# Assembling the attention output of a two-layer hybrid diffusion trunk: two ScalarE copies and one GpSimd add for each half-copied, half-added pair on ScalarE and VectorE

## The chip, the cores and the metric

The kernel runs on one core of one Trainium2 chip. The metric is the device time of one execution in microseconds (us); lower is better. The kernel before takes 2939.41 us, the median of three runs (2939.0 to 2944.37).

## The reference

The reference is a trunk of two layers over 1024 latent tokens and 256 context tokens, 1024 features wide, batch 1, in float32. Layer 0 mixes tokens with a convolution module, layer 1 with grouped-query attention (16 query heads, 4 key/value heads, 64 features each). After each of the two stands a SwiGLU feed-forward network (FFN) with 2816 hidden features. What the change touches is the attention of layer 1, for the latent tokens:

```python
qg = q.reshape(B, Q, N_KV_HEADS, KV_GROUP, Dh)
s = jnp.einsum("bqkgd,bskd->bkgqs", qg, k).astype(jnp.float32) * (Dh ** -0.5)
p = jax.nn.softmax(s, axis=-1).astype(v.dtype)
o = jnp.einsum("bkgqs,bskd->bqkgd", p, v)
...
yx = ob.transpose(1, 0, 2, 3).reshape(B, S, N_HEADS * HEAD_DIM) @ wo
```

The 1024 queries read all 1280 keys (latent and context).

## The kernel before

**Number format.** Large products are made from pairs. A float32 number is split into a high part (rounded to the matmul's faster format) and a low part (the remainder), and a product is the sum of high x high, high x low and low x high. ScalarE makes the high part by a copy, VectorE the low part by a subtraction. TensorE (PE in the profile) does all products and the transposes; its results lie in the eight banks of PSUM, which GpSimd does not read anywhere in this kernel.

**Attention, one unit at a time.** The work of attention is cut into 32 units. A unit is one key/value head with its four query heads, for 128 queries. The scores of a unit (`scores`, line 1105) take 24 matmuls (L1116: four heads, 1280 keys in pieces of 512 and 256, high and low part of the keys). For each head VectorE scales the 1280 scores of a query, takes their minimum and writes them to SBUF (L1122), and ScalarE takes the exponential with the sum beside it (L1124).

The values of a unit (`values`, line 1128) go through the 1280 keys in ten tiles of 128. For each tile PE transposes the four heads' probabilities into one bank (L1134, four instructions), ScalarE copies the high part out of it (L1137), VectorE subtracts to get the low part (L1138), and PE multiplies both by the values (L1140 with the high part, L1141 with the low part) and sums all ten tiles up in one bank, number 7, called `av`. Two banks take the transposes in turn while attention runs alone, one while it shares the core; four slots hold the high and low parts, so at most four tiles can be ahead of the multiplications.

**Putting the output together.** The values' weights hold the high parts of the 64 value features in 64 columns and their low parts in the other 64, so `av` holds in its lower 64 partitions the part of the output that comes from the high parts, and in its upper 64 the part from the low parts, for four heads of 128 queries. The output of a unit is the sum of the two, laid out as 128 partitions (two heads x 64 features) by two by 128 queries, and then divided by the softmax's sums. For each half of the partitions, ScalarE copies one part from `av` to the scratch tile `tmp`, moving it across partitions (L1151, 64 x 256 numbers), and VectorE adds the other part, read from `av`, to it and writes the output tile `dst` (L1152). The reciprocal of the sums is taken by VectorE (L1145), spread out by GpSimd (L1147), transposed by PE into bank 7 (L1155, two instructions, called the two small transposes below), and VectorE multiplies the output by it (L1156). GpSimd then issues the DMA that writes the unit's output to memory (L1450). The last unit of each half of the queries writes to a tile of its own, `olast`, with no DMA. Bank 7 has to be read out by all of this before the next unit's first L1140 may write to it.

**What sets the order.** The Python code is a set of generators that a tile framework's scheduler then lists engine by engine, by its own cost model and by priorities; `later(40)` gives the L1140 and L1141 a lower priority. Each engine executes its list strictly in order and waits at an instruction until the instructions that it depends on are done. So a change of one instruction can change the whole list. GpSimd's list also holds the DMA issues: a unit's queries (L1102), keys (L1095), outputs (L1450), and the loads for the output projection (L1485, L1500).

**Stages of the second layer.** From about 1565 us the first 16 units (queries 0 to 511) start beside the last query/key projections (`qkv`); from about 1640 to 1862 us they run alone. Then the output projection of the first half (`out_proj`, from line 1481) starts on these units' output, and the other 16 units (queries 512 to 1023) run beside it and, from about 1965 us, beside the FFN of the first half, until 2393 us. The rest is the second half's output projection and FFN.

Of the kernel before, what the change touches and what calls it, by code (L numbers as in the profile page):

```python
# [12 lines left out]
ALU = mybir.AluOpType  # L13
# [42 lines left out]
class Kern:  # L56
# [1071 lines left out]
    def values(self, t, Ps, sums, dst, done):  # L1128
        nc, c = self.nc, self.c
        av = self.bank("av")  # L1130
        for j in range(NJ):
            tp = self.bank("pt")
            for h in range(4):
                nc.tensor.transpose(tp[:, h * P:(h + 1) * P], Ps[h][:, j * P:(j + 1) * P], c["ident"])  # L1134
            ph, pl = self.ptring[self.ptslot % len(self.ptring)]
            self.ptslot += 1
            nc.scalar.copy(ph, tp)  # L1137
            nc.vector.tensor_tensor(pl, tp, ph.bitcast(F32), op=ALU.subtract)  # L1138
            with self.later(self.lav):
                nc.tensor.matmul(av, lhsT=self.value(t, j), rhs=ph, start=j == 0, stop=False)  # L1140
                nc.tensor.matmul(av, lhsT=self.value(t, j), rhs=pl, start=False, stop=j == NJ - 1)  # L1141
            yield 0.87

        r = sums[:, 1, :]
        nc.vector.reciprocal(r, sums[:, 0, :])  # L1145
        rx = self.sb(256)
        nc.gpsimd.tensor_copy(rx.rearrange("p (h d) -> p h d", d=HD), r.unsqueeze(2).to_broadcast([P, 4, HD]))  # L1147
        tmp = self.sb(256).rearrange("p (a q) -> p a q", q=P)
        v = av.rearrange("p (a b q) -> p a b q", b=2, q=P)
        for b, r, o in ((0, slice(0, 64), slice(64, 128)), (1, slice(64, 128), slice(0, 64))):  # L1150
            nc.scalar.copy(tmp[r], v[o, :, b, :])  # L1151
            nc.vector.tensor_tensor(dst[r], v[r, :, b, :], tmp[r], op=ALU.add)  # L1152
        rb = self.bank("av")
        for a in range(2):
            nc.tensor.transpose(rb[:, a * P:(a + 1) * P], rx[:, a * P:(a + 1) * P], c["ident"])  # L1155
        nc.vector.tensor_tensor(dst, dst, rb[:, 0:256].rearrange("p (a q) -> p a q", q=P), op=ALU.mult)  # L1156
        done()
        yield 0.1
# [565 lines left out]
```

## Time and profile before

| what | value |
|---|---|
| time, median of 3 runs | 2939.41 us |
| time of the profiled execution | 2938.98 us |
| its span, first to last instruction | 2937.2 us |
| mean granted PE clock in it | 0.987 |
| busy: PE, VectorE (DVE), ScalarE (ACT), GpSimd (POOL) | 97%, 74%, 45%, 8% |
| L1151, ScalarE's copies | 64, 23.5 us in all |
| L1152, VectorE's adds | 64 (60 to scratch tiles, 4 to `olast`) |
| L1147, GpSimd's spreading copies | 32, 13.8 us in all |

All times inside the kernel are counted from the start of the span. In rows that group instructions, the columns are: line, engine, operation, output<-input by the program's names with their shapes, count, then busy time in us and mean duration of one in ns, then idle time of the engine just before them in us and what ended most of it. In rows of a timeline, the columns are: start in us, duration in us, engine, line, operation, output<-input, count, and in brackets the idle time of the engine just before it and what ended it. PE is the stream of matmuls, PEld that of the weight loads ahead of them. Matmuls overlap in the pipeline, so the distance between the starts of two neighbours says what one costs, and not its duration.

### The profile page before, as it was taken

The page shows a single profiled execution, that of the slowest core. Times are in us where ns is not written, and L with a number is a line of the kernel's source. Part 1 is how long each engine was busy: PE and PEld are TensorE (multiplying, and loading weights), DVE is VectorE, ACT ScalarE, POOL GpSimd, SP SyncE. Part 2 cuts the span into 40 slices and gives each one's busy share as a digit, 9 for nine tenths or more (in the row PEclk, how much of TensorE's full clock was granted, in tenths as well). Part 3 has the DMA queues.
Part 4 walks back from the last instruction along what each step waited for, and adds up shares of the span by engine and source line. Part 5 has one row for each costly group of instructions (what it writes and reads, how often), then busy time and mean ns, then how long its engine had stood idle before and what let it go on. Part 6 is the DMA issues. An engine that isn't in the chain of part 4 may idle for free.

```text
span 2937.2 us, 42731 instructions
## 1 busy us (share of the span) xinstructions
PE 2847.7 (97%) x16462; PEld 2446.1 (83%) x16462; DVE 2160.7 (74%) x3746; ACT 1335.5 (45%) x2229; POOL 222.6 (8%) x377
## 2 busy tenths in 40 slices
PE   7999989999999999999999999989999999999998
PEld 6888877888888889989888787767777778889997
DVE  6887788847556378877786899786666666786777
ACT  5222255532222245544445688645555543444444
POOL 0000001011022001000011111110000000010000
PEclk9999999999999999999999999999999999999999
DMA  6443444334356224333345211322222143353332
GB/s 249 140 120 98 116 131 145 135 116 143 115 175 198 65 74 165 114 104 112 109 156 170 88 46 46 97 87 81 66 73 83 60 149 99 110 170 104 102 98 75
DMA packets 131755, 336.58 MB, mean 115 GB/s; under 512 B 31328, under 2 KB 52864, under 8 KB 130656
## 3 DMA queue, kind: packets, MB, share of 16 engines
q1 hardware_dynamic: 78016, 222.33, 24.1%
q0 software_dynamic: 29344, 103.83, 10.7%
q10 hardware_dynamic: 24192, 7.70, 1.1%
q8 instruction: 129, 2.11, 0.3%
q14 instruction: 74, 0.61, 0.1%
HBM read 289.50 MB, written 38.93 MB: 112 GB/s over the span
## 4 chain that ended last, share of the span: by engine, by line
PE 86%; DVE 7%; ACT 2%; issue 2%; DMA 2%; ACTq 0%; POOL 0%; SPq 0%; DVEq 0%; POOLq 0%
PE ps L172 15%; PE ps L173 15%; PE ps L174 15%; PE ps L875 4%; PE ps L877 4%; PE ps L876 4%; PE ps L1116 4%; PE ps L1134 4%; PE ps L1140 2%; PE ps L454 2%; PE ps L455 2%; PE ps L456 2%; PE ps L1141 2%; PE ps L185 1%; PE ps L183 1%
## 5 line engine op out<-in xcount | busy, mean ns | idle before, releaser
L172 PE MATMUL ps<-T,wh 128*128 128x512 f32 (+1 forms) x1360 | 502.5, 370 | 1.4 <-ACT T L161 0.8
L174 PE MATMUL ps<-T,wl 128*128 128x512 f32 (+1 forms) x1360 | 500.4, 368 | 2.0 <-DVE wl L148 2.0
L173 PE MATMUL ps<-T,wh 128*128 128x512 f32 (+1 forms) x1312 | 481.4, 367 | 0.2 <-DVE T L164 0.2
L144 ACT CAST wh<-wr 128x1024 fp32r<-128x1024 f32 (+1 forms) x217 | 225.0, 1037 | 419.9 <-PE ps L173 307.2
L148 DVE TENSOR_TENSOR wl<-wr,wh 128x1024 fp32r<-128x1024 f32 (+1 forms) x217 | 261.9, 1207 | 168.5 <-ACT wh L144 167.1
L875 PE MATMUL ps<-T,wh 128*128 128x256 f32 x1092 | 310.7, 285 | 5.0 <-ACT wh L161 4.5
L876 PE MATMUL ps<-T,wh 128*128 128x256 f32 x1092 | 306.5, 281 | 0.0
L877 PE MATMUL ps<-T,wl 128*128 128x256 f32 x1092 | 305.4, 281 | 0.2 <-DVE wl L164 0.2
L1138 DVE TENSOR_TENSOR T<-ps,T 128x512 fp32r<-128x512 f32 x320 | 216.8, 687 | 107.6 <-ACT T L1137 106.8
L172 PEld LDWEIGHTS ps<-T,wh 128*128 128x128 f32 x1360 | 257.8, 190 | 43.7 <-ACT T L1506 1.7
L174 PEld LDWEIGHTS ps<-T,wl 128*128 128x128 f32 x1360 | 257.7, 190 | 42.4 <-DVE wl L148 2.2
L173 PEld LDWEIGHTS ps<-T,wh 128*128 128x128 f32 x1312 | 248.5, 189 | 38.2 <-DVE T L164 1.3
L1137 ACT CAST T<-ps 128x512 fp32r<-128x512 f32 x320 | 186.0, 586 | 191.1 <-PE ps L1134 177.6
L173 PE MATMUL ps<-HS,wh 128*128 128x512 f32 x656 | 257.9, 393 | 0.0
L172 PE MATMUL ps<-HS,wh 128*128 128x512 f32 x608 | 238.4, 392 | 0.9 <-ACT wh L144 0.9
L174 PE MATMUL ps<-HS,wl 128*128 128x512 f32 x608 | 237.5, 391 | 0.0
L875 PEld LDWEIGHTS ps<-T,wh 128*128 128x128 f32 x1092 | 206.1, 189 | 11.2 <-ACT wh L161 6.7
L876 PEld LDWEIGHTS ps<-T,wh 128*128 128x128 f32 x1092 | 206.6, 189 | 0.5
L877 PEld LDWEIGHTS ps<-T,wl 128*128 128x128 f32 x1092 | 206.2, 189 | 0.6 <-DVE wl L164 0.4
L1134 PE MATMUL ps<-cst,T 128*128 128x128 f32 x1100 | 189.6, 275 | 3.2 <-DVE T L1138 3.1
L1122 DVE TENSOR_SCALAR_CACHE_REDUCE T<-ps,rq 128x1280 f32<-128x1280 f32 x110 | 170.0, 1546 | 27.9 <-PE ps L1116 22.1
L1134 PEld LDWEIGHTS ps<-cst,T 128*128 128x128 f32 x1100 | 132.6, 141 | 49.5 <-DVE T L1138 30.8
(377 smaller groups left out, 6195.9 us busy)
## 6 DMA issues: line engine op xcount, KB each, us to landing
wr<-in_w SPq DMA_DIRECT2D x170, 512.0 KB, 3.6
wr<-in_pw SPq DMA_DIRECT2D x35, 512.0 KB, 3.5
HV<-in_wmodT POOLq DMA_DIRECT2D x56, 256.0 KB, 4.1
q<-in_wmodT POOLq DMA_DIRECT2D x56, 256.0 KB, 3.9
KB<-in_w SPq DMA_DIRECT2D x24, 512.0 KB, 3.6
HR<-in_w SPq DMA_DIRECT2D x23, 512.0 KB, 3.7
q<-in_w SPq DMA_DIRECT2D x23, 512.0 KB, 4.2
q<-qsd POOLq DMA_DIRECT2D x32, 256.0 KB, 3.3
```

The costliest lines, as they stand in the source:

```text
L144: nc.scalar.copy(hi, raw)
L148: nc.vector.tensor_tensor(lo, raw, hi.bitcast(F32), op=ALU.subtract)
L172: nc.tensor.matmul(out[:, :n], lhsT=wh, rhs=xh, start=k == 0, stop=False)
L173: nc.tensor.matmul(out[:, :n], lhsT=wh, rhs=xl, start=False, stop=False)
L174: nc.tensor.matmul(out[:, :n], lhsT=wl, rhs=xh, start=False, stop=k == nk - 1)
L875: nc.tensor.matmul(out, lhsT=wh, rhs=bh, start=first and k == 0, stop=False, **skip)
L876: nc.tensor.matmul(out, lhsT=wh, rhs=bl, start=False, stop=False, **skip)
L877: nc.tensor.matmul(out, lhsT=wl, rhs=bh, start=False, stop=k == 3, **skip)
L1122: nc.vector.tensor_scalar(out=pt, in0=sc, scalar1=rq[:, h:h + 1], scalar2=None, op0=ALU.mult, op1=ALU.min, accum_out=mn)
L1134: nc.tensor.transpose(tp[:, h * P:(h + 1) * P], Ps[h][:, j * P:(j + 1) * P], c["ident"])
L1137: nc.scalar.copy(ph, tp)
L1138: nc.vector.tensor_tensor(pl, tp, ph.bitcast(F32), op=ALU.subtract)
```

## The change

In `values`, the first of the two parts is still copied by ScalarE into `tmp`. The second is no longer added by VectorE on its way out of the bank: ScalarE copies it to `dst` as well, for both halves of the partitions, and then one GpSimd instruction over all 128 partitions adds `tmp` to `dst`, both in SBUF. For a unit, that is four copies on ScalarE and one add of 128 x 256 on GpSimd where there were two copies on ScalarE and two adds of 64 x 256 on VectorE.

```diff
         for b, r, o in ((0, slice(0, 64), slice(64, 128)), (1, slice(64, 128), slice(0, 64))):
             nc.scalar.copy(tmp[r], v[o, :, b, :])
-            nc.vector.tensor_tensor(dst[r], v[r, :, b, :], tmp[r], op=ALU.add)
+            nc.scalar.copy(dst[r], v[r, :, b, :])
+        nc.gpsimd.tensor_tensor(dst, dst, tmp, op=ALU.add)
         rb = self.bank("av")
```

Lines below it move down by one: in the changed kernel L1152 is the second copy, L1153 the add, L1156 the small transposes (L1155 before), L1157 the multiplication (L1156 before), and L1451 the output's DMA (L1450 before).

The scheduler lists the engines anew. Three places show it, all without the number of the row.

**VectorE, at the end of a unit while attention runs alone.** Names: `T_13571` holds the slots of high and low parts, `HS`, `T_13569` and `T_14068` (`T_14069` after) the probabilities, `sb` the scratch and output tiles. Before:

```order
L1122 TENSOR_SCALAR T_13569,mn<-ps,rq_10629 128x1280
L1138 TENSOR_TENSOR T_13571<-ps,T_13571 128x512
L1152 TENSOR_TENSOR sb<-ps,sb 64x256
L1138 TENSOR_TENSOR T_13571<-ps,T_13571 128x512
L1122 TENSOR_SCALAR HS,mn<-ps,rq_10629 128x1280
L1152 TENSOR_TENSOR sb<-ps,sb 64x256
L1138 TENSOR_TENSOR T_13571<-ps,T_13571 128x512
L1156 TENSOR_TENSOR sb<-sb,ps 128x256
L1122 TENSOR_SCALAR T_13569,mn<-ps,rq_10629 128x1280
```

The same unit's end after:

```order
L1138 TENSOR_TENSOR T_13571<-ps,T_13571 128x512 x2
L1122 TENSOR_SCALAR HS,mn<-ps,rq_10629 128x1280
L1138 TENSOR_TENSOR T_13571<-ps,T_13571 128x512 x2
L1145 RECIPROCAL sums<-sums 128x4
L1157 TENSOR_TENSOR sb<-sb,ps 128x256
L1122 TENSOR_SCALAR T_13569,mn<-ps,rq_10629 128x1280
```

The two adds are gone, and the multiplication stands nearer to the unit's last subtraction: one pass over the scores lies between where there were two.

**PE, at the same unit's end.** `HR` and `HV` are the values, `KB` the keys, `cst` the identity of the transposes; the first row's L1141 is the unit's last multiplication, and the next unit's first one is an L1140. Before:

```order
L1141 MATMUL ps<-T_13571,HR 128x512
L1116 MATMUL ps<-KB,q 128x512 x4
L1116 MATMUL ps<-KB,q 128x256 x2
L1116 MATMUL ps<-KB,q 128x512 x2
L1134 MATMUL ps<-cst,T_13569 128x128
L1134 MATMUL ps<-cst,T_14068 128x128 x3
L1116 MATMUL ps<-KB,q 128x512 x2
L1134 MATMUL ps<-cst,T_13569 128x128
L1134 MATMUL ps<-cst,T_14068 128x128 x3
L1116 MATMUL ps<-KB,q 128x256 x2
L1116 MATMUL ps<-KB,q 128x512
L1155 MATMUL ps<-cst,sb 128x128 x2
```

After (the next unit's L1140 is the last row; before, it stands behind two more score matmuls and three more transposes):

```order
L1141 MATMUL ps<-T_13571,HR 128x512
L1116 MATMUL ps<-KB,q 128x512
L1116 MATMUL ps<-KB,q 128x256 x2
L1116 MATMUL ps<-KB,q 128x512 x2
L1134 MATMUL ps<-cst,T_13569 128x128
L1134 MATMUL ps<-cst,T_14069 128x128 x3
L1156 MATMUL ps<-cst,sb 128x128 x2
L1116 MATMUL ps<-KB,q 128x512
L1134 MATMUL ps<-cst,T_13569 128x128
L1134 MATMUL ps<-cst,T_14069 128x128 x3
L1140 MATMUL ps<-T_13571,HV 128x512
```

The small transposes stand after five score matmuls and four transposes where 13 and eight preceded them, and the next unit's first multiplication after six and eight where 15 and 11 preceded it.

**GpSimd, at the end of the first unit.** Before:

```order
L1102 DMA q<-qsd 128x4x128
L1450 DMA od<-sb 128x2x128
L1102 DMA q<-qsd 128x4x128
L1147 COPY sb<-sums 128x256 x2
L1450 DMA od<-sb 128x2x128
```

After:

```order
L1102 DMA q<-qsd 128x4x128
L1153 ISA
L1153 TENSOR_TENSOR sb<-sb 128x256
L1147 COPY sb<-sums 128x256
L1451 DMA od<-sb 128x2x128
L1102 DMA q<-qsd 128x4x128
L1147 COPY sb<-sums 128x256
L1153 TENSOR_TENSOR sb<-sb 128x256
L1451 DMA od<-sb 128x2x128
```

An add stands ahead of each output DMA, and ahead of the first add one more instruction, `ISA`, which tells GpSimd to load the library of code that the add is in; it stands there once.

## The prediction

> **What bounds the kernel now.** The page first, for the share of each engine:
>
> ```profile
> PE 2847.7 (97%) x16462; PEld 2446.1 (83%) x16462; DVE 2160.7 (74%) x3746; ACT 1335.5 (45%) x2229; POOL 222.6 (8%) x377
> ```
>
> PE is busy nearly throughout, so VectorE's 74% says little: what an add less on VectorE is worth depends on whether PE waits there. The adds lie in the second layer's attention, so I cut that into stages with the windows view (columns: stretch, its length, busy us and count of PE, PEld, DVE, ACT, POOL, then granted clock, DMA share, GB/s):
>
> ```profile
> 1640.00:1865.00 225.00, 215.06 (x1281) 174.13 (x1280) 202.94 (x335) 180.24 (x304) 33.93 (x55) 1.00 0.19 53
> 1965.00:2385.00 420.00, 419.31 (x2155) 329.73 (x2154) 278.47 (x407) 229.06 (x357) 29.76 (x47) 1.00 0.26 77
> ```
>
> These are two different kernels. In the first stretch attention runs alone: VectorE is busy 90% of it, ScalarE 80%, and PE has gaps. In the second PE has FFN matmuls to fill every gap and waits 0.7 us in 420; VectorE has a third of its time free. A gain can come from the first stretch only. Its groups over eight units, with shapes kept apart, show who is close to the limit:
>
> ```profile
> L1138 DVE TENSOR_TENSOR T<-ps,T 128x512 fp32r<-128x512 f32 x82 | 54.6, 685 | 8.3 <-ACT T L1137 8.1
> L1137 ACT CAST T<-ps 128x512 fp32r<-128x512 f32 x80 | 46.1, 587 | 19.8 <-PE ps L1134 12.3 <-PE ps L1140 4.9
> ...
> L1152 DVE TENSOR_TENSOR sb<-ps,sb 64x256 f32<-64x256 f32 x16 | 6.7, 416 | 0.2
> ...
> L1151 ACT COPY sb<-ps 64x256 f32<-64x256 f32 x16 | 5.9, 368 | 0.4
> ...
> L1156 DVE TENSOR_TENSOR sb<-sb,ps 128x256 f32<-128x256 f32 x8 | 3.3, 410 | 0.0
> L1147 POOL COPY sb<-sums 128x256 f32<-128x256 f32 x8 | 3.2, 399 | 8.9 <-DMA od<-sb 4.4 <-issue 3.7 <-POOL sb L1147 0.6
> ```
>
> VectorE's idle time in front of its main step (8.3 us in eight units) is spent waiting for ScalarE's high parts, and ScalarE's (19.8 us) waiting for PE: a ring of three engines with short queues, none of them at its limit. The chain of waits gives the pace, by two score passes at the same place of the pattern eight units apart:
>
> ```profile
> 1702.22 1.16 PE ps L1116 x6
> ...
> 1819.87 1.17 PE ps L1116 x6
> ```
>
> That is 117.65 / 8 = 14.71 us a unit. What PE alone would need comes from the spacing of neighbours in the timeline:
>
> ```profile
> 1731.47 1.32 PE L1116 MATMUL ps<-KB,q 128*128 128x512 f32 x6
> ...
> 1732.63 1.03 PE L1134 MATMUL ps<-cst,T 128*128 128x128 f32 x8
> ...
> 1733.42 0.48 PE L1141 MATMUL ps<-T,HR 128*128 128x512 f32 x1
> ...
> 1739.85 0.40 PE L1141 MATMUL ps<-T,HV 128*128 128x512 f32 x1
> ...
> 1740.09 0.39 PE L1140 MATMUL ps<-T,HR 128*128 128x512 f32 x1
> ```
>
> Six score matmuls take 1.16 us, eight transposes 0.79, one multiplication 0.24. A unit has four times the first (4.64), five times the second (3.95), 20 of the third (4.8) and two small transposes of 0.1: 13.6 us. So PE loses 1.1 us a unit here, and no change on another engine can win more than that.
>
> **What goes, what comes, and what is moved.** The stretch holds the ends of units 0 to 14, so 14 distances of a unit. The end of a unit, between its last multiplication and the next unit's first, reads now:
>
> ```profile
> 1734.36 0.37 ACT L1151 COPY sb<-ps 64x256 f32<-64x256 f32 x1
> 1734.63 1.36 ACT L1124 ACTIVATE T<-T,mn 128x1280 f32<-128x1280 f32 x1
> 1734.91 0.40 DVE L1152 TENSOR_TENSOR sb<-ps,sb 64x256 f32<-64x256 f32 x1
> ...
> 1735.84 1.53 DVE L1122 TENSOR_SCALAR_CACHE_REDUCE HS<-ps,rq 128x1280 f32<-128x1280 f32 x1
> ...
> 1736.11 0.36 ACT L1151 COPY sb<-ps 64x256 f32<-64x256 f32 x1
> ...
> 1737.41 0.43 DVE L1152 TENSOR_TENSOR sb<-ps,sb 64x256 f32<-64x256 f32 x1
> ...
> 1738.01 0.39 PE L1155 MATMUL ps<-cst,sb 128*128 128x128 f32 x2
> ...
> 1738.47 0.41 DVE L1156 TENSOR_TENSOR sb<-sb,ps 128x256 f32<-128x256 f32 x1
> ...
> 1738.80 1.54 DVE L1122 TENSOR_SCALAR_CACHE_REDUCE T<-ps,rq 128x1280 f32<-128x1280 f32 x1
> ...
> 1738.94 0.50 PE L1140 MATMUL ps<-T,HV 128*128 128x512 f32 x1
> ```
>
> The two copies and two adds take turns, and an exponential and a pass over the scores slip in between, so bank 7 is held from 1733.42 to 1738.94, 5.5 us.
>
> *Gone:* two adds of 0.416 a unit, 0.83 us of VectorE's busy time. Neighbours overlap by 0.08 (0.41 from 1738.47 on, the next at 1738.80), so I count, with one overlap left out, 0.75 us of VectorE's time a unit.
>
> *Added on ScalarE:* two copies of 0.368. The one above lets its neighbour start 0.27 after it, so four in a row take 3 x 0.27 + 0.37 = 1.18 us, 0.54 more than two. ScalarE is idle 19.8 / 8 = 2.5 us a unit in front of L1137 alone; that covers it. If that cover fails, an exponential comes up to 0.54 later.
>
> *Added on GpSimd:* one add of 128 x 256. The trace has no GpSimd add. The nearest row from below is L1147, a copy of the same shape, one input: 0.40. Two inputs read in turn would be 0.80. I take 0.65, nearer to the upper end, since there are two inputs. [...]
>
> *The chain at a unit's end after.* From the start of the last multiplication to the first copy:
>
> ```profile
> 1863.83 0.40 PE L1141 MATMUL ps<-T,HR 128*128 128x512 f32 x1
> ...
> 1864.26 0.37 ACT L1151 COPY sb<-ps 64x256 f32<-64x256 f32 x1 [0.38 <-PE ps L1141]
> ```
>
> 0.43, then four copies 1.18, then about 0.05 for each hand-over: the small transposes can start at 1.66, the add at 1.66 as well, the multiplication at 1.66 + 0.65 + 0.05 = 2.36, the next unit's first L1140 at 2.36 + 0.41 + 0.05 = 2.8. PE has, by the order shown, six score matmuls (four wide, two narrow: 1.18), eight transposes (0.8) and the two small ones (0.2) in between, 2.2 us behind the 0.24 of the last multiplication. So PE waits 2.8 - 2.4 = 0.4 us there. The order runs in a cycle of three units; at the other two ends, by the same count, there are 3.3 and 3.65 us of matmuls, and PE doesn't wait. That is 0.12 us a unit.
>
> VectorE waits too, since L1157 stands in its queue in front of the next scores and subtractions, and it is reached early: at the end shown one pass of 1.54, two subtractions of 0.685, each less the overlap of 0.08, and a reciprocal (0.1) lie between the unit's last subtraction and it, 2.8 us. The last multiplication starts 0.7 after that subtraction (one tile's transposes, 0.4, and an L1140 go ahead of it), so the multiplication could start 0.7 + 2.36 = 3.1 after it: a wait of 0.3. ScalarE, however, has two L1137 in front of the four copies, which can push them back by up to 0.9. I take the long end, 1.2, because both L1137 wait for an exponential that ends just before: 0.4 us a unit over the cycle of three. At the other two ends two passes over the scores lie between, and the product is ready in time.
>
> Gain a unit: 0.75 - 0.4 - 0.12 = 0.23, say 0.2; over 14 units **-2.8 us**. Bounds: the whole 0.75, so -10.5, if neither wait occurs; +1, if the small waits come at each end.
>
> *At the end of the stretch.* The output of unit 14 goes to memory and comes back for the output projection, and ScalarE and PE wait for it:
>
> ```profile
> 1860.72 0.83 ACT L161 CAST T<-HS 128x768 fp32r<-128x768 f32 x1 [2.05 <-DMA HS<-od]
> ...
> 1862.09 0.50 PE L1140 MATMUL ps<-T,HR 128*128 128x512 f32 x1 [1.18 <-ACT T L1137]
> ```
>
> Unit 14's multiplication now stands ahead of two subtractions that preceded it, so its DMA leaves earlier; of PE's 1.18 I count half: **-0.5** (between 0 and -1.2).
>
> *Once: the library.* GpSimd is free before the first add:
>
> ```profile
> 1637.80 0.77 POOL L1102 DMA_DIRECT2D q<-qsd  x1 [0.61 <-PE ps L1134]
> 1648.04 0.71 POOL L1450 DMA_DIRECT2D od<-sb  x1 [9.47 <-DVE sb L1156]
> ```
>
> ```profile
> 1642.64 0.37 ACT L1151 COPY sb<-ps 64x256 f32<-64x256 f32 x1
> ```
>
> From 1638.57 on it may load, and the first add is due when four copies from 1642.64 on are done, at 1643.8: 5.2 us. No row shows such a load. The nearest are ScalarE's table load and, as the long end, the median landing of a 512 KB DMA:
>
> ```profile
> L1124 ACT ACT_TABLE_LOAD x1 | 1.3, 1283 | 0.0
> ```
>
> ```profile
> q<-in_w SPq DMA_DIRECT2D x23, 512.0 KB, 4.2
> ```
>
> With 1.3 to 4.2 us it is hidden: **0**. If it took longer, each us more would hold the first output, its multiplication in VectorE's queue, and so PE. [...]
>
> *Beside the FFN.* PE is full, so VectorE's relief brings nothing in these 14 unit ends. What can cost is that the small transposes now stand closer behind the last multiplication, in most units after some 1.4 us of matmuls. They need the four copies: 1.66 against 0.24 + 1.4 = 1.64. The row for them before shows that they wait a little already, beside other matmuls:
>
> ```profile
> L1155 PEld LDWEIGHTS ps<-cst,sb 128*128 128x128 f32 x28 | 2.9, 141 | 3.2 <-issue 2.7 <-POOL sb L1147 0.3
> ```
>
> I take 0.05 us an end, **+0.7**; bounds 0, and 0.3 an end (+4.2), if ScalarE is in the middle of an exponential of 1.37 at one end in five. GpSimd's queue holds the adds behind query loads (L1102), which wait for the scores two units back; those stand ahead of the small transposes on PE, so no add waits for one. L1450 and the loads behind it come as late as the add makes them, and nobody waits for an output DMA but the last of each half.
>
> Sum: -2.8 - 0.5 + 0 + 0.7 = -2.6 us. Against the profiled execution, 2938.98 us with a span of 2937.2, this is 2936.4; that execution is 0.43 below the median of the three runs, so I forecast **2936.8 us** for the median.
>
> **The rivals.** About 0.2%, 5.9 us, is what a measurement of this kernel tells from no change.
>
> *VectorE's relief is kept whole.* If VectorE is what paces the ring, the unit shrinks by all of 0.75, which PE's 1.1 of slack allows: -10.5 - 0.5, or 2928.4 us. For it speaks VectorE's 90% and that the exchange over bank 7 falls from 5.5 to some 3 us; against it, that VectorE's idle time is spent waiting for ScalarE, which gets more work. Chance 0.20, counting from 2933.5 down.
>
> *GpSimd's add becomes the wait (the other side).* The chain copies, add, multiplication, next L1140 has no slack at one end in three and 0.9 to 1.2 us at the others. If the add takes 1.4 us instead of 0.65 and hand-overs to and from GpSimd 0.2 each, the chain is 3.9 us and PE loses 1.5, 0.4 and 0 at the three ends, 0.63 a unit, while VectorE waits some 1.0 a unit: a unit is 0.9 longer, over 14 units +12, so 2951 us. It decides from an add of about 1.0 us on, where VectorE's waits eat the 0.75. Against it stands L1147 with 0.40. Chance 0.09.
>
> *ScalarE's copies hold up PE beside the FFN.* If the four copies come behind an exponential of 1.37 at most of the 14 ends, PE waits 0.7 at each, +10, and with -3.3 from the other stage the time is 2946 us. ScalarE is busy 229 of 420 us there, which makes it possible, but the order places them where ScalarE is expected free. Chance 0.05, the long library load included.
>
> That the change does not do what it says is ruled out by the order: 128 copies and 32 adds stand in it.
>
> **How the numbers follow.** The forecast, a time within 5.9 us of 2939.4, has 0.66; of its range, the gain of 10.5 is cut in half and the loss of 4.2 taken beside no gain, so 2933.5 to 2943.5. To hold 8 in 10, the range goes down into the first rival, to 2930; 2943.5 leaves out the two slower ones. Faster by over 0.2%: 0.20. Within 0.2%: 0.66. Slower: 0.09 + 0.05 = 0.14.
>
> **What would show it.** Right: 14.4 to 14.6 us a unit between 1700 and 1820; the add at 0.5 to 0.8 us; VectorE idle for L1157 at one unit end in three, for GpSimd; PE's busy time beside the FFN still within 1% of the stretch; a gap on GpSimd before its first add, over before 1643.8. Wrong: a unit under 14.0 (VectorE did pace the ring), a unit over 14.7 or VectorE waiting for the add at every end (GpSimd is the new wait), or PE waiting for the small transposes by more than 0.3 us each beside the FFN.

## The result and the profile after

The changed kernel takes **2949.41 us**, the median of 11 runs (2945.95 to 2953.03); the kernel before, run beside it, 2940.61 us (2938.53 to 2944.37). The ratio is 1.003 (95% interval 1.0022 to 1.0038): slower by 8.8 us, where I had forecast 2936.8 us, a gain of 2.6. The profiled execution after took 2946.87 us, with a span of 2945.1 us, 7.9 us longer than that of before (2937.2).

The two stages first, by the windows view (columns as in the prediction: stretch, its length, busy us of PE, PEld, DVE, ACT, POOL, granted clock, DMA share, GB/s):

```profile
1640.00:1865.00 225.00, 213.36 (x1268) 173.18 (x1268) 189.20 (x299) 187.84 (x331) 46.31 (x72) 1.00 0.20 55
1965.00:2385.00 420.00, 414.87 (x2128) 326.02 (x2127) 266.38 (x377) 237.13 (x382) 39.05 (x60) 1.00 0.26 76
```

VectorE is relieved in both (202.94 to 189.20, and 278.47 to 266.38). But PE, which was busy 419.31 of 420 us beside the FFN, is now busy 414.87: the stage in which PE had no gap has gaps of 5 us. The waits view names them; first alone (1640 to 1865), then beside the FFN (1990 to 2390). Columns: waiting engine and line, releaser, us in all, times, longest.

```profile
PE ps L1156 <- ACT sb L1152: 6.7, 14, 0.8
...
PE ps L1140 <- DVE sb L1157: 0.7, 4, 0.2
```

```profile
PE ps L1156 <- ACT sb L1152: 4.0, 12, 0.4
```

The second is the only PE wait that the view lists in those 400 us; before, it lists none. L1156 are the small transposes: PE reaches them while ScalarE is still copying `av` out of bank 7, which they write. The timeline shows one such end beside the FFN:

```profile
2071.18 0.48 PE L1141 MATMUL ps<-T,HR 128*128 128x512 f32 x1
...
2071.74 0.37 ACT L1151 COPY sb<-ps 64x256 f32<-64x256 f32 x1 [0.70 <-issue]
...
2072.13 0.37 ACT L1152 COPY sb<-ps 64x256 f32<-64x256 f32 x1
...
2072.88 0.37 ACT L1152 COPY sb<-ps 64x256 f32<-64x256 f32 x1
2073.28 1.37 ACT L1124 ACTIVATE T<-T,mn 128x1280 f32<-128x1280 f32 x1
2073.39 0.41 PE L1156 MATMUL ps<-cst,sb 128*128 128x128 f32 x2 [0.35 <-ACT sb L1152]
...
2074.16 0.42 DVE L1157 TENSOR_TENSOR sb<-sb,ps 128x256 f32<-128x256 f32 x1 [1.47 <-POOL sb L1153]
```

The first copy starts 0.56 us behind the last multiplication, the copies start 0.38 apart and don't overlap (the last L1152 is the fourth copy: 1.51 us for all four), and the small transposes come 2.2 us behind the last multiplication, 0.35 of which PE stands still. The exponential (L1124), whose input VectorE finished at 2072.7, waits behind the copies until 2073.28. VectorE waits 1.47 us for the add, but nothing of PE's stands behind that here.

At the same place the kernel before has the two copies apart, with an exponential between them; ScalarE waits 0.18 us ahead of the first copy and 0.65 behind it, so that one lies in a gap:

```profile
2066.97 0.37 ACT L1151 COPY sb<-ps 64x256 f32<-64x256 f32 x1 [0.18 <-PE ps L1141]
2067.99 1.37 ACT L1124 ACTIVATE T<-T,mn 128x1280 f32<-128x1280 f32 x1 [0.65 <-DVE T L1122]
...
2069.47 0.36 ACT L1151 COPY sb<-ps 64x256 f32<-64x256 f32 x1
```

Where the 7.9 us of the two spans came from is read by the same instruction in both kernels at five places: the first unit's multiplication, the output projection's first square (L390), the FFN's first product (L839), a group of eight tiny matmuls (L746, each one column wide) in the second norm (its first group, HS, is for the clock, below), and the end. The first three rows are of the timeline, the other two of the view by line (duration in ns: least, median, most; then first and last start). Before:

```profile
1647.34 0.41 DVE L1156 TENSOR_TENSOR sb<-sb,ps 128x256 f32<-128x256 f32 x1
...
1883.70 0.64 ACT L390 ACTIVATE sb<-T 128x512 f32<-128x512 f32 x1
...
1966.66 0.68 DVE L839 SCALAR_TENSOR_TENSOR sm<-sm,ps 128x512 f32<-128x512 f32 x1
```

```profile
L746 PE MATMUL ps<-cst,HS x8: 250/250/250, 1933.2 to 1934.0; 128*128 128x1 f32 x8
...
L746 PE MATMUL ps<-cst,HV x8: 250/250/250, 2480.9 to 2481.7; 128*128 128x1 f32 x8
```

After:

```profile
1644.92 0.41 DVE L1157 TENSOR_TENSOR sb<-sb,ps 128x256 f32<-128x256 f32 x1
...
1883.92 0.64 ACT L390 ACTIVATE sb<-T 128x512 f32<-128x512 f32 x1
...
1969.43 0.68 DVE L839 SCALAR_TENSOR_TENSOR sm<-sm,ps 128x512 f32<-128x512 f32 x1
```

```profile
L746 PE MATMUL ps<-cst,HS x8: 352/352/352, 1935.1 to 1936.6; 128*128 128x1 f32 x8
...
L746 PE MATMUL ps<-cst,HV x8: 250/250/250, 2488.0 to 2488.8; 128*128 128x1 f32 x8
```

| stretch | difference at its end | lost in it |
|---|---|---|
| up to the first unit's multiplication | -2.4 | -2.4 |
| alone, with the stage's last unit end, to the first L390 | +0.2 | +2.6 |
| output projection and norm, to the first L839 | +2.8 | +2.6 |
| beside the FFN, to the second L746 | +7.1 | +4.3 |
| the rest | +7.9 | +0.8 |

The first row is not the change's. PE's matmuls stand in the same order in both kernels up to the last multiplication of the first unit, and ahead of it one and the same L1140, first before and then after, comes 2.4 us earlier:

```profile
1633.39 0.51 PE L1140 MATMUL ps<-T,HR 128*128 128x512 f32 x1 [0.45 <-ACT T L1137]
```

```profile
1631.01 0.50 PE L1140 MATMUL ps<-T,HR 128*128 128x512 f32 x1 [0.45 <-ACT T L1137]
```

The lead is 2.4 us at 1548 us already, before the first unit begins, so this execution was ahead by that much for reasons that the change doesn't touch. At the first unit's last multiplication on PE (L1141) it is 3.4 (1641.75 before, 1638.34 after); counted from there the second row is 3.6, not 2.6. From the L1140 on, this pair of profiles differs by 10.3 us, where the medians differ by 8.8.

PE's clock has a part in the rows. In the norm the eight HS matmuls last 352 ns instead of 250. The windows view has the granted clock; before, over three stretches of some 10 us:

```profile
1632.00:1642.00 10.00, 8.11 (x30) 6.21 (x31) 8.01 (x21) 5.13 (x7) 2.22 (x3) 0.66 0.35 131
...
1930.00:1941.00 11.00, 9.94 (x58) 8.00 (x57) 8.91 (x29) 4.16 (x8) 0.00 (x0) 0.84 0.17 55
...
2486.00:2496.00 10.00, 10.00 (x48) 8.14 (x47) 9.72 (x27) 4.58 (x7) 1.68 (x3) 1.00 0.38 131
```

After:

```profile
1632.00:1642.00 10.00, 8.13 (x37) 5.84 (x37) 7.47 (x18) 6.86 (x12) 3.29 (x5) 0.83 0.36 131
...
1930.00:1941.00 11.00, 10.10 (x48) 8.34 (x47) 8.31 (x22) 4.42 (x8) 0.00 (x0) 0.69 0.24 79
...
2486.00:2496.00 10.00, 10.00 (x52) 8.53 (x52) 5.54 (x26) 1.63 (x2) 0.00 (x0) 0.83 0.18 55
```

The two traces hold no other clock than 1 and one half, so this is 6.8, 3.5 and 0 us at half clock before, and 3.4, 6.8 and 3.4 after. At half clock PE's matmuls of 128x512 start 0.43 us apart (2490.27 to 2492.83 after), at the full clock 0.23 (2484.91 to 2486.04), so PE loses at most half of each, and the clock can have given 1.7 us in the first place (the lead grew by 1.0 there) and taken 1.7 in each of the other two. But all stretches at half clock of the two spans add up to 78 us before and 76 after, so the 7.9 as a whole can't be put down to the clock. The largest piece of the loss lies beside the FFN, where the granted clock is 1.00 throughout.

### The profile page after: what moved, and what is told of

Its sections match the earlier page's. It is cut to its first block, busy times and chain, and to the rows that moved or that the text cites. A ratio compares the mean times of both kernels' runs of the same rounds, so it can differ in the third digit from the quotient of the medians.

```text
span 2945.1 us, 42741 instructions
## 1 busy us (share of the span) xinstructions
PE 2849.6 (97%) x16462; PEld 2447.8 (83%) x16462; DVE 2137.4 (73%) x3682; ACT 1357.2 (46%) x2293; POOL 245.8 (8%) x409
## 5 line engine op out<-in xcount | busy, mean ns | idle before, releaser
L1138 DVE TENSOR_TENSOR T<-ps,T 128x512 fp32r<-128x512 f32 x320 | 215.6, 688 | 125.5 <-ACT T L1137 125.3
L1134 PE MATMUL ps<-cst,T 128*128 128x128 f32 x1100 | 189.5, 275 | 3.1 <-DVE T L1138 3.1
L1122 DVE TENSOR_SCALAR_CACHE_REDUCE T<-ps,rq 128x1280 f32<-128x1280 f32 x110 | 170.2, 1548 | 30.6 <-PE ps L1116 24.6
L1134 PEld LDWEIGHTS ps<-cst,T 128*128 128x128 f32 x1100 | 132.7, 141 | 47.5 <-DVE T L1138 28.3
```

The lines of the kernel that those rows point to most:

```text
L1122: nc.vector.tensor_scalar(out=pt, in0=sc, scalar1=rq[:, h:h + 1], scalar2=None, op0=ALU.mult, op1=ALU.min, accum_out=mn)
```

## The experiments

Theory A, from the profile above: the loss comes from four ScalarE copies between a unit's last multiplication and the small transposes, which PE reaches too early. Theory B, the rival: the GpSimd add makes VectorE wait (8.1 us alone, 13.2 beside the FFN), and PE behind it. "Alone" and "beside" in the code are told by the ring of score regions, `sring`.

**One stage at a time.**

```diff
+            if self.sring != [TOK]:
                 nc.scalar.copy(dst[r], v[r, :, b, :])
+            else:
+                nc.vector.tensor_tensor(dst[r], v[r, :, b, :], tmp[r], op=ALU.add)
...
+        if self.sring != [TOK]:
+            nc.gpsimd.tensor_tensor(dst, dst, tmp, op=ALU.add)
```

> The new form only for units that end while two score regions are in use (from some 1640 us to the FFN), the old form for the rest. Theory A (the loss lies beside the FFN, where PE reaches the small transposes 1.4 us behind the last multiplication and waits for four ScalarE copies; the stage alone nets nothing): 2938 to 2942 us, and no PE wait at the small transposes between 1990 and 2390 us. Theory B (the GpSimd add makes VectorE, and PE behind it, wait at each unit's end, mostly alone): 2946 to 2950 us.

Measured: 2954.34 us, ratio 1.0049 (1.0036 to 1.0061). Beside the FFN, as theory A says, nothing is lost:

```profile
1990.00:2390.00 400.00, 399.96 (x2057) 315.06 (x2057) 264.61 (x389) 218.67 (x341) 28.33 (x45) 1.00 0.26 77
```

But alone it loses far more than the changed kernel did, 15.6 us a unit (see the table below), though the instructions at each end are the same on the same engines. What differs is the list: the scheduler, which lists the two stages together, now repeats the shortest of the three unit ends of the changed kernel at every unit, with 2.2 us of matmuls between a unit's last multiplication and the next one's first. PE waits for the small transposes (7.8 us), VectorE for GpSimd (15.1 us at 11 ends):

```profile
PE ps L1160 <- ACT sb L1153: 7.8, 14, 0.6
```

```profile
DVE sb L1161 <- POOL sb L1157: 15.1, 11, 1.4
```

So theory B is not empty: alone, with this list, VectorE waits for the add at 11 ends and a unit is 0.9 us longer than before. The time agrees with neither number. The reverse has `==` for `!=`:

> The reverse: the new form only for the units that end beside the FFN, the old form alone; beside the FFN the list of PE has the same distances as after the change. Theory A: most of the loss is here, 2945 to 2949 us, with PE waiting at the small transposes for ScalarE about 0.35 us at each of 12 ends or more between 1990 and 2390 us, and PE's busy time there 4 us lower than before. Theory B: 2940 to 2942 us, since VectorE has a third of its time free there.

Measured: 2945.94 us, ratio 1.0018 (1.0009 to 1.0027), as theory A says: the form beside the FFN takes most of the loss by itself. Beside the FFN PE stands at the small transposes (L1160 here) for the same 4.0 us at 12 ends:

```profile
PE ps L1160 <- ACT sb L1153: 4.0, 12, 0.4
```

**The add on VectorE, or the copy on VectorE.** These take apart the two things that the change adds.

```diff
-        nc.gpsimd.tensor_tensor(dst, dst, tmp, op=ALU.add)
+        nc.vector.tensor_tensor(dst, dst, tmp, op=ALU.add)
```

> ScalarE copies both halves as after the change, but VectorE adds the two from SBUF: no GpSimd add, no library. PE's list still has the small transposes 1.4 to 1.9 us behind the last multiplication beside the FFN. Theory A: PE still waits there for ScalarE, and the time stays at 2945 to 2949 us. Theory B: with GpSimd out of the chain the loss goes, 2940 to 2942 us.

Measured: 2947.43 us, ratio 1.0028 (1.0017 to 1.004). Without any GpSimd add the loss is there, and PE's gaps beside the FFN with it (busy 395.55 of 400 us):

```profile
1990.00:2390.00 400.00, 395.55 (x2034) 309.94 (x2033) 254.11 (x368) 224.09 (x360) 27.91 (x44) 1.00 0.25 74
```

The other half: ScalarE with its two copies as before, VectorE copying where it added, GpSimd adding.

```diff
-            nc.scalar.copy(dst[r], v[r, :, b, :])
+            nc.vector.tensor_copy(dst[r], v[r, :, b, :])
```

> ScalarE copies one half as before, VectorE copies the other (where it added before), GpSimd adds: the add is there, the two further ScalarE copies are not. PE's list has 2.5 to 6.8 us of matmuls ahead of the small transposes again. Theory A: no PE wait over 0.5 us in all at the small transposes beside the FFN, nothing lost there, 2939 to 2944 us. Theory B: the add is in the chain and VectorE has no relief, 2947 to 2953 us.

Measured: 2959.79 us, ratio 1.0068 (1.0055 to 1.0081). Beside the FFN the GpSimd add costs nothing:

```profile
1990.00:2390.00 400.00, 399.76 (x2055) 314.99 (x2054) 266.15 (x391) 218.62 (x341) 38.55 (x60) 1.00 0.26 77
```

Alone it costs 1.6 us a unit, and the time is above what either theory said; VectorE copies there where it added before, and the GpSimd add comes on top. So the two stages have two answers. Beside the FFN the ScalarE copies cost and the add does not. Alone the kernels with the add on GpSimd take 14.8 to 16.3 us a unit, with VectorE relieved (14.8, and 15.6 in the first experiment) or not (16.3), and what in their lists sets these paces is not shown.

**Moving the small transposes away.** If PE only comes too early, they can be listed later:

```diff
-            nc.tensor.transpose(rb[:, a * P:(a + 1) * P], rx[:, a * P:(a + 1) * P], c["ident"])
+            with self.later(100):
+                nc.tensor.transpose(rb[:, a * P:(a + 1) * P], rx[:, a * P:(a + 1) * P], c["ident"])
```

> The changed kernel with the small transposes at a lower priority, so that PE's list has 1.5 to 3.1 us of matmuls ahead of them beside the FFN (1.4 to 1.9 in the changed kernel) and 2.9 us alone (1.3); copies and GpSimd add are as after. Theory A (PE reaches them before ScalarE's four copies are done): PE's waits there between 1990 and 2390 us fall from 4.0 to under 1 us, the FFN stretch loses at most 1.5 us instead of 3 to 4, PE doesn't wait there alone either, and the time is 2939 to 2944 us, some 5 below after. Theory B (the GpSimd add and VectorE's wait for it): nothing of that is removed, 2946 to 2951 us.

Measured: 2949.05 us, ratio 1.0035 (1.0022 to 1.0049): nothing is won, and theory A falls in the form in which I had it. The waits at the small transposes (L1157 here) did go, but others came:

```profile
1990.00:2390.00 400.00, 395.65 (x2037) 311.35 (x2036) 250.87 (x358) 225.44 (x364) 39.91 (x58) 1.00 0.26 75
...
PE ps L1134 <- ACT T L1124: 2.3, 6, 0.5
PE ps L1157 <- ACT sb L1152: 1.0, 3, 0.4
PE ps L1134 <- DVE T L1138: 0.9, 3, 0.4
```

PE now waits with the next unit's transposes (L1134) for an exponential. One such place in the timeline:

```profile
2103.77 0.37 ACT L1152 COPY sb<-ps 64x256 f32<-64x256 f32 x1
2104.16 1.36 ACT L1124 ACTIVATE T<-T,mn 128x1280 f32<-128x1280 f32 x1
...
2105.67 0.33 PE L1134 MATMUL ps<-cst,T 128*128 128x128 f32 x1 [0.28 <-ACT T L1124]
```

VectorE's pass over the scores for this exponential ran from 2101.24 to 2102.79; the exponential starts at 2104.16, right behind the last of four copies that began at 2102.63. The same with VectorE adding:

```diff
-        nc.gpsimd.tensor_tensor(dst, dst, tmp, op=ALU.add)
+        nc.vector.tensor_tensor(dst, dst, tmp, op=ALU.add)
...
+            with self.later(100):
```

> ScalarE copies both halves, VectorE adds from SBUF, and the small transposes at the lower priority: 1.4 to 3.1 us of matmuls ahead of them beside the FFN, 1.8 alone. Theory A: PE's waits beside the FFN fall from 4.4 (the same without the lower priority) to under 1 us, and the time from 2947 to 2938 to 2943 us. If the lower priority does nothing, 2946 to 2949.

Measured: 2950.6 us, ratio 1.0042 (1.0029 to 1.0054): a miss again, with PE busy 395.50 of the 400 us and waiting for L1124 (2.2 us), the copies (1.3) and L1138 (0.9). So the kernel with the later transposes took a time that theory B had named, but not for its reason: the loss is the same without a GpSimd add.

**Another bank.** Beside the FFN the lower half of bank 2 is free, and the small transposes could go there, where no copy has to be waited for:

```diff
-        rb = self.bank("av")
+        rb = self.ps[:, 2, :] if self.sring == [TOK] else self.bank("av")
```

> The changed kernel, but the small transposes of the units beside the FFN write to the free half of bank 2, so they need no copy out of bank 7. Theory A: PE's waits at them between 1990 and 2390 us go from 4.0 to 0 us (1.2 us at the half-clock norm steps may come or go), and the time falls by 4 us or more against after, to 2941 to 2946 us. Theory B: VectorE still waits for the add, and the time stays at 2948 to 2951 us.

Measured: 3034.56 us, ratio 1.0323 (1.0309 to 1.0337). The waits at the small transposes are gone, but the upper half of bank 2 belongs to the scores, and the next unit's scores now wait for the multiplication that reads the lower half:

```profile
PE ps L1116 <- DVE sb L1157: 8.5, 12, 0.9
```

VectorE waits there for the add, 29.4 us at 12 ends, and the list holds the scores back as well. Attention then ends so late that PE has too little beside it: from 2390 to 2490 us it is busy 70.71 of 100 us, at a mean clock of 0.76. It tells nothing on the theories.

**Theory A, second form**: not ScalarE's time and not PE's place costs, but the block of four copies in a row, 1.5 us in which neither bank 7 nor the next exponential moves on. Then as much ScalarE work in two pieces, with an exponential between, should be free. The kernel before, with two spare copies a unit beside the FFN:

```diff
             nc.scalar.copy(tmp[r], v[o, :, b, :])
             nc.vector.tensor_tensor(dst[r], v[r, :, b, :], tmp[r], op=ALU.add)
+            if self.sring == [TOK]:
+                nc.scalar.copy(spare[r], tmp[r])
```

> The kernel before, with two more ScalarE copies of 64 x 256 for each unit beside the FFN, from the scratch tile to a spare one: as much ScalarE time as the change adds, but bank 7 isn't read by them, and PE's list keeps 2.4 to 5.2 us ahead of the small transposes. If ScalarE's time as such holds up PE (the exponential behind the copies is late): PE's busy time between 1990 and 2390 us falls from 400.0 to some 396 and the time rises by 3 to 5 us. If the place is what costs (four copies between the last multiplication and what PE does next, with bank 7 held): PE stays at 399 to 400, and the time within 2 us of before.

Measured: 2941.07 us, ratio 1.0006 (0.9997 to 1.0015). ScalarE is as busy as after the change (226.53 against 224.03), and PE has no gap:

```profile
1990.00:2390.00 400.00, 399.77 (x2059) 314.34 (x2058) 261.53 (x384) 226.53 (x363) 29.25 (x46) 1.00 0.26 75
```

Its copies (L1152) and spare ones (L1155) stand in pairs on either side of an exponential (the second spare copy follows at 2071.94):

```profile
2069.02 0.37 ACT L1152 COPY sb<-ps 64x256 f32<-64x256 f32 x1 [0.18 <-PE ps L1141]
2069.43 0.41 ACT L1155 COPY sb<-sb 64x256 f32<-64x256 f32 x1
2070.06 1.36 ACT L1124 ACTIVATE T<-T,mn 128x1280 f32<-128x1280 f32 x1 [0.23 <-DVE T L1122]
...
2071.54 0.36 ACT L1152 COPY sb<-ps 64x256 f32<-64x256 f32 x1
```

The spare copies differ from the change's in two ways, the place and that they don't read bank 7, so this shows that ScalarE's time as such is free, and not which half of the second form weighs more.

**The changed kernel again**, unaltered, for a second profile.

> The changed kernel once more, for a second profile: 2947 to 2952 us. If the half-clock stretches of PE around 1635, 1935 and 2490 us fall by chance and not by the change, they lie elsewhere relative to the work than in the first profile: the first unit's multiplication then differs by 1 us or more between the two profiles, and the pace alone (14.77 us a unit) and PE's waits beside the FFN (4.0 us) don't.

Measured: 2951.07 us, ratio 1.0036 (1.0023 to 1.0049). Pace and waits repeat (4.0 us at 12 ends, PE busy 395.90 of 400). The half-clock stretches repeat as well: the first unit's multiplication came at 1645.42, 0.5 from the first profile, and the stretches in the three places lasted 3.4, 6.8 and 3.4 us again. That they fall by chance is not shown. Nor is it shown that the change causes them: the kernel with the spare copies, which takes the time of before, has 6.8 us in the second place and 3.4 in the third as well, and the kernel with the new form beside the FFN only, which is slower than before, has 3.4 and none. What the clock adds stays open.

**Can both be beaten?** The old form beside the FFN, and alone ScalarE's four copies with VectorE's one add (the diff of the first experiment, with `nc.vector` in the last line):

> The old form beside the FFN; for the units that end alone, ScalarE copies both halves and VectorE adds them from SBUF in one instruction of 128 x 256. If the loss beside the FFN is that of the ScalarE copies there, it is gone: PE 399 to 400 us busy between 1990 and 2390. Alone the pace is 14.58 us a unit, as with VectorE adding everywhere, 0.13 under before, less 1 to 2 us at the last unit end of the stage: 2937 to 2941 us. If the loss of the changed kernel has another source than those two, 2945 us and up.

Measured: 2942.45 us, ratio 1.0011 (1.0002 to 1.0019), a little above the range. PE is busy 399.95 of 400 us again: what was lost beside the FFN is the copies'. With the small transposes of the units alone at `later(150)`:

> The same with the small transposes of the units that end alone at a lower priority (2.9 us of matmuls ahead of them instead of 1.8), so that PE doesn't wait there for ScalarE. If those waits of 0.33 us at each end alone cost time: 14.3 us a unit and 2934 to 2938 us. If PE only waits elsewhere instead, as happened with the lower priority beside the FFN: 14.6 to 14.9 us a unit and 2938 to 2944 us.

Measured: 2946.44 us, ratio 1.0023 (1.0013 to 1.0033), above both ranges; PE's waits at the small transposes are gone, and the pace is 14.9 us a unit, longer than with them (14.6). And with the old form for the seventeenth unit, by asking for `"mm" not in self.banks` in place of `self.sring != [TOK]`:

> As the kernel with ScalarE copying both halves and VectorE adding only for the units that end alone, but without the seventeenth unit, which ends beside the output projection: there the old form stays, and PE's list has 6.3 us ahead of its small transposes, not 3.0. In the run before, that unit's end turned a lead of 4.1 us over the kernel before into a lag of 0.3. If that loss is the form's, the lead is kept: 2936 to 2940 us, at or below before. If it is work that only stands elsewhere in the list: 2941 to 2944 us.

Measured: 2941.45 us, ratio 1.0008 (0.9999 to 1.0017). Its lead over the kernel before was 2.8 us at the first L390, of which 1.4 was there at the first unit's last multiplication, up to which PE's order is that of before; it was 0.1 at the sixth and 0.5 at the seventh. So the lead is mostly work that stands elsewhere in the list. No version beats the kernel before.

The pace alone, from the starts of two multiplications 8 units apart (9 for the changed kernel, whose ends repeat every three). The matmul time ahead is worked out from the lists with the spacings of the prediction:

| who copies, who adds | matmuls ahead of the small transposes, us | from, to | us a unit |
|---|---|---|---|
| before | 3.4 | 1709.07, 1826.7 | 14.70 |
| after | 1.3 to 1.4 | 1704.96, 1838.14 | 14.80 |
| after's form alone only | 1.3 | 1711.0, 1835.6 | 15.6 |
| after, later transposes | 2.9 | 1708.7, 1827.8 | 14.9 |
| ScalarE both, VectorE adds | 1.8 | 1705.1, 1821.8 | 14.6 |
| the same, later transposes | 2.9 | 1710.4, 1829.5 | 14.9 |
| ScalarE and VectorE copy, GpSimd adds | 2.9 to 3.6 | 1712.8, 1843.2 | 16.3 |

With equal distances of 2.9 GpSimd's add and VectorE's give the same pace. But the two kernels at 1.3 with the same instructions at a unit's end are 0.8 us apart, and the one at 2.9 to 3.6 is the slowest, so this distance doesn't set the pace alone; what does, and why 1.8 is better than 2.9, stays open.

## Why the prediction was wrong

**The step that failed is the term beside the FFN.** I put PE's wait at the small transposes at 0.05 us an end, +0.7 in all; it is 0.33 at 12 ends, 4.0 us, and the stretch lost 4.3. The place was right, the size was not, and it came from the chain: I had the first copy at 0.43 and four copies in 1.18, so 1.66, against 1.64 of matmuls. Measured are 0.56, 1.51 and 0.12, together 2.2. The 1.18 rested on one neighbour that started 0.27 behind a copy (1734.36 to 1734.63); between copies it is 0.38. My bound, "0.3 an end (+4.2)", came close to the value, but I took it for a rare case, an exponential in the way, when it follows from the copies alone: at ten of the 13 ends between 1990 and 2390 us the first copy starts 0.43 to 0.57 behind the last multiplication.

**The same wait was left out in the stage alone, and the sum is further off there.** I asked only when the next L1140 could start, and PE does wait little for that (0.7 us at 4 ends). At the small transposes it waits 6.7 us at 14 ends. The gain of 0.2 us a unit, -2.8 in all, became a loss of 0.09 a unit, 14 x 0.09 = +1.3, and with the last unit end of the stage +2.6, where -3.3 was forecast: 5.9 off, against 3.6 beside the FFN. That this wait ate the gain is not shown, since with the small transposes later a unit took 14.9 us. With the measured waits a unit in place of my terms (VectorE 0.58 for the add, PE 0.48 at the small transposes and 0.05 at L1140) my sum would give a loss of 0.36, four times what came, so adding up the waits of several engines, as my sum does, gives too much. In the stage's last unit end the other step, "unit 14's DMA leaves earlier" (-0.5), came true and was then lost again:

```profile
1859.22 0.83 ACT L161 CAST T<-HS 128x768 fp32r<-128x768 f32 x1 [0.84 <-DMA HS<-od]
...
1864.54 0.41 PE L1156 MATMUL ps<-cst,sb 128*128 128x128 f32 x2 [0.35 <-ACT olast L1152]
...
1865.22 1.55 DVE L1122 TENSOR_SCALAR_CACHE_REDUCE T<-ps,rq 128x1280 f32<-128x1280 f32 x1 [1.51 <-PE ps L1116]
```

ScalarE's wait for the DMA fell from 2.05 to 0.84, and 5 us later PE waits at the small transposes, the scores stand behind them in its list, and VectorE idles 1.51 us. That these waits are what took the lead is read from the rows and not tested.

**A stretch I had not costed** is the output projection, where the seventeenth unit ends: at its last square (L390, 1929.40 before, 1930.53 after) the lag is 1.1 us, 0.9 more than at the first. The further 1.6 us up to the first L839 are about what the longer half-clock stretch there can take.

**What held.** The add was put at 0.65 us and took 0.73; the table of groups gives a mean of 764 ns, which one instruction of 1358 pulls up:

```profile
L1153 POOL TENSOR_TENSOR sb<-sb 128x256 f32<-128x256 f32 x30 | 22.9, 764 | 170.4 <-ACT sb L1152 120.6 <-issue 49.8
```

VectorE was to wait 1.2 us for the add at one unit end in three; it waited at 7 ends of 15, 1.16 us each:

```profile
DVE sb L1157 <- POOL sb L1153: 8.1, 7, 1.6
```

GpSimd's library was put at nothing, and no row shows that it cost anything, or that one was loaded. The best row is that of the kernel with the form alone only, where the last work of GpSimd ahead of the first add ends at 1659.80 and MODIFY_POOL_CONFIG, which the trace has at the add's line where the list has `ISA`, stands at 1659.8:

```profile
1659.40 0.40 POOL L1147 COPY sb<-sums 128x256 f32<-128x256 f32 x1 [7.52 <-DVE sums L1145]
1661.33 0.73 POOL L1157 TENSOR_TENSOR sb<-sb 128x256 f32<-128x256 f32 x1 [1.52 <-ACT sb L1153]
```

If there was a load, it fits into the 1.52 us there, and ScalarE is what ended the wait. Whether there was one in this execution is not shown.

**The rivals.** The one that came is the third, ScalarE's copies holding up PE beside the FFN, which I gave 0.05, with the argument that "the order places them where ScalarE is expected free". It came by another way than I gave: PE waits 0.33 an end, not 0.7, and at most ends no exponential stands ahead of the copies. The argument is the error: the order is what the scheduler expects, and it listed the small transposes 1.4 to 1.9 us of matmuls behind the last multiplication, where the chain takes 2.2. That its cost model has the four copies too short would explain this, but that model is not on record. The kernel before has the longer exchange over bank 7, but its list leaves 2.3 us or more of matmuls ahead of the small transposes, and so nobody waits. The second rival, the add as the wait, came only in part in the changed kernel (8.1 us of VectorE's waits), and at the size I gave it, 0.9 us a unit, where the list repeats the shortest end (15.6), though the add takes 0.73 and not 1.4. VectorE's relief was not kept whole anywhere: the best pace seen, 14.6 us a unit, is 0.1 under before, not 0.75.

Of the signs named for a wrong forecast, two came: a unit over 14.7 us, and PE's waits of more than 0.3 us each beside the FFN.

## What to carry to other kernels

Where one engine is full, count for each of its waits the time that its list leaves in front of it against the measured chain, from as many rows as there are; a change can make the scheduler list the waiting instruction closer behind its chain, and so make it wait for the first time. Several short instructions in a row on an engine that others wait for have to be counted as one block: ScalarE's four copies of 0.37 us took 1.51 us here and, with bank 7 held, cost PE 4.0 us, while as much ScalarE work in two pieces was free (2941.07 us). And a wait that is moved away has to be followed to the next one in the queue before it counts as a gain.

## What the runs showed of the hardware

ScalarE's copies of 64 x 256 from PSUM, 0.37 us each, start 0.38 us apart when they follow each other: they don't overlap.

GpSimd's add of 128 x 256 from SBUF, two inputs, takes 0.73 us where its copy of the same shape (L1147) takes 0.40.

PE's granted clock fell to one half for 3.4 or 6.8 us in the norm's tiny matmuls and after, and in one place while PE was busy without a gap: in the stretch from 2486 to 2496 us after, shown above, PE is busy 10.00 of 10 us at a mean clock of 0.83. The half clock lasts 3.4 us there, from 2489.9 us on, and PE is busy 3.40 of 3.40 us both in it and in the 3.4 us ahead of it. The stretches at half clock of the two traces last 3.4 us or two, three or four times that, but for the last of each (15.1 us before, 13.5 after).
